# Loading and modulating a second group of rows earlier in a streaming-encoder step

## The chip, the cores and the metric

The kernel runs on one core of one Trainium2 chip. The metric is the device time of one execution in microseconds (us), the median of several runs. Nothing else runs on the chip.

## What is computed

One layer of a hybrid encoder on 1024 prompt rows and 64 sample rows of width 1024, cut here to what the change touches:

```python
sh1, sc1, ga1, sh2, sc2, ga2 = split(silu(c) @ w_ada + b_ada, 6)   # adaLN; one c for the prompt, one for the sample
h   = rmsnorm(x, g_pre_mix) * (1.0 + sc1) + sh1
u   = h @ w_in                      # columns [diff q | diff k | diff v | sb q | sb k | sb v]
mix = concat(differential attention (4 head pairs), stick-breaking attention (8 heads))
x   = x + ga1 * rmsnorm(mix @ w_out, g_post_mix)
x   = x + ga2 * rmsnorm(relu(h2 @ w_up) ** 2 @ w_down, g_post_ffn)  # h2 as h, with sh2 and sc2
```

The keys and values of the new rows are outputs too.

## The kernel before, in words

The 1088 rows are nine tiles of 128 (x0 to x7 of the prompt, x8 the 64 sample rows), in three groups: x0 to x2 are group 0, x3 to x5 group 1, x6 to x8 group 2. All large products run in split form: a number is stored as a high part and a remainder, and one product takes three matmuls (lines 303 to 305: high by high, high by low, low by high).

The first 100 us are the ones that matter here. SyncE (SP) issues all loads on one queue, in this order: `w_ada`, the adaLN weights, of which the first half of the columns is needed here, in four quarters q of four pieces of 512 KB (`ada_raw`, L128; tiles `ar` and `ae`), mixed with x0 to x2 and with three weight tiles of `w_in`; then x3 to x8 (`load_x`, L114, called at L405); then the lambda vectors, two tables (`Tst0`, `T0`) and the next weights (`wq1r`, `wk1r`).

`norm_inplace` (L153) scales a row tile by its inverse RMS: two squares with a sum on ScalarE (L87), three small operations on GpSimd (L89, L80, L81), two multiplications on VectorE (L158). The shift and scale vectors of adaLN come quarter by quarter: each quarter is 16 small matmuls into a bank `pam` (L201), a copy `Rm` to SBUF (L322), four matmuls into `pcm` (L209) and three operations on VectorE that write the columns A1 and B1 (L326 to L328, `columns`). Quarter q gives the columns for the blocks k = 2q and 2q+1, where a block is 128 of the 1024 columns.

`block_T(g, k, tag)` (L330) transposes block k of group g's three row tiles on TensorE into one PSUM bank `px` (`px06` is block 6 of group 0, `px10` block 0 of group 1). `block_mod` (L338) applies A1 and B1 to it (even blocks on VectorE, L346; odd ones on ScalarE, L344) and splits the result into the high part `h1h` (ScalarE, L64) and the remainder `h1l` (L65: on VectorE for group 0, on GpSimd for the others). `first(k)` (L357) multiplies block k of group 0 with the first three weight tiles, nine matmuls into three banks `p00`, `p01`, `p02` that stay open over all eight blocks.

The loop at L383 goes over the four quarters, with the modulation of one quarter running between the matmuls of the next. After it come `first(4)` to `first(7)`, the loads of x3 to x8, the projections of group 0, and then `ready_1` (L579, called at L1006): the norms of x3 to x5 and the eight blocks of group 1. The projections of group 1 (`pq01`, `pk01`, `pv01`) and the first attention steps (`pz`) follow; the blocks of group 2 are made inside the projection of group 1 (`proj`, L563).

The program order isn't the order on the engines: the kernel is built with a scheduler that places each instruction by its own estimate of when its inputs are there. Each engine then executes the order that it was given, and a load on SP first waits for a counter: eight counters are used in turn, so each load waits until the load eight places before it has landed.

A bank is one of two of its tag ("tr", "qk", "pv", "pj"). While `p00` to `p02` are open, each of the first three tags has one bank left, so a `px` has to be read before the next one of its tag can be written.

Of the kernel before, what the change touches and what calls it, by code (L numbers as in the profile page):

```python
# [18 lines left out]
KT = D // P  # L19
# [8 lines left out]
NTT = 9  # L28


def fr(ap):
    return ap.bitcast(F32)


def build(tc, I, O):
    nc = tc.nc
# [10 lines left out]
    def big(name, tag, shape, dt=F32R):  # L47
        return sb.tile(shape, dt, tag=tag, name=name, bufs=BUFS[tag])

    def small(shape, name, tag, dt=F32, bufs=2):  # L50
        return sb.tile(shape, dt, tag=tag, name=name, bufs=bufs)
# [4 lines left out]
    def bank(name, tag):  # L56
        return pp.tile([P, 512], F32, tag=tag, name=name)
# [4 lines left out]
    def split(src, hi, lo, eh=None, el=None):  # L62

        (eh or nc.scalar.copy)(hi, src)  # L64
        (el or nc.vector).tensor_tensor(lo, src, fr(hi), ALU.subtract)  # L65

    def halves(name, n=2):
        return [big(f"{name}_{i}", "s", [P, 512], F32) for i in range(n)]
# [9 lines left out]
    def rstd(ss, rows, name, add=EPS, inv=1.0 / D):  # L78
        r = small([P, 1], name, "rs", bufs=4)
        nc.gpsimd.tensor_scalar(r[:rows], ss, inv, add, ALU.mult, ALU.add)  # L80
        nc.gpsimd.tensor_tensor(r[:rows], r[:rows], mhalf[:rows], ALU.pow)  # L81
        return r

    def sumsq(srcs, rows, name, scratch):
        ss = small([P, 2], name, "ss", bufs=4)
        for i, (a, jk) in enumerate(zip(srcs, scratch)):
            nc.scalar.activation(jk[:rows, : a.shape[-1]], a, AF.Square, accum_out=ss[:rows, i : i + 1])  # L87
        if len(srcs) == 2:
            nc.gpsimd.tensor_tensor(ss[:rows, 0:1], ss[:rows, 0:1], ss[:rows, 1:2], ALU.add)  # L89
        return ss[:rows, 0:1]  # L90
# [5 lines left out]
    def x_rows(m):  # L96
        return (x_p[m * P : (m + 1) * P, :], P) if m < 8 else (x_s, TS)
# [16 lines left out]
    def load_x(m):  # L114
        src, rows = x_rows(m)
        x = big(f"x{m}", "qk" if m < 8 else "v", [P, 1024], F32)
        load(x[:rows], src)
        return [x[:, :512], x[:, 512:]]
# [9 lines left out]
    def ada_raw(q, part, half):  # L128
        n = 4 * q + 2 * part + half
        if n < 10:  # L130
            raw = big(f"ar{q}{part}{half}", "qk", [P, 4, 256], F32)
        else:
            raw = eh[(n - 10) // 3][:, (n - 10) % 3]
        c0 = D * part + 256 * q
        load(raw, w_ada[:, 4 * half : 4 * half + 4, c0 : c0 + 256])
        ada_raws[c0, half] = raw
# [9 lines left out]
    xn = []  # L146
# [6 lines left out]
    def norm_inplace(xs, m):  # L153
        rows = x_rows(m)[1]
        jk = [small([P, 512], f"jk{m}{i}", "ah") for i in range(2)]
        r = rstd(sumsq([x[:rows] for x in xs], rows, f"ssa{m}", jk), rows, f"rsa{m}")
        for x in xs:
            nc.vector.tensor_scalar(x[:rows], x[:rows], r[:rows], None, ALU.mult)  # L158
# [126 lines left out]
    def drain(gen):  # L285
        for _ in gen:
            pass
# [10 lines left out]
    def dense_T(ps, w, act, g, ks=range(KT)):  # L298

        n = GRP[g][1]  # L300
        (wh, wl), (hh, hl) = w, act[g]
        for k in ks:
            mm(ps[:, :n], lhsT=wh[:, k, :], rhs=hh[:, k, :n], start=(k == 0), stop=False)  # L303
            mm(ps[:, :n], lhsT=wh[:, k, :], rhs=hl[:, k, :n], start=False, stop=False)  # L304
            mm(ps[:, :n], lhsT=wl[:, k, :], rhs=hh[:, k, :n], start=False, stop=(k == 7))  # L305
            yield 3 * n / 2400
# [4 lines left out]
    def proj_weights(u, i):  # L311
        c = unit_cols(u)[i]
        return weights(w_in[:, :, c : c + P], [P, KT, P], f"w{'qkv'[i]}{u}", el=nc.vector if u == 0 else None)
# [16 lines left out]
    def block_T(g, k, tag):  # L330

        ps = bank(f"px{g}{k}", tag)
        for m in range(3 * g, 3 * g + 3):
            rows, off = x_rows(m)[1], (m % 3) * P
            nc.tensor.transpose(ps[:, off : off + rows], xn[m][k // 4][:rows, (k % 4) * P : (k % 4 + 1) * P], ident[:rows, :rows])
        return ps

    def block_mod(ps, g, k, el=None, on_act=False):  # L338
        n = GRP[g][1]
        xt = small([P, 512], f"xt{g}{k}", "al")  # L340
        for j, c in ((0, slice(0, min(n, TP - GRP[g][0]))), (1, slice(256, 320)))[: 1 + (g == 2)]:
            a, b = A1[:, k, j : j + 1], B1[:, k, j : j + 1]
            if on_act and j == 0:
                nc.scalar.activation(xt[:, c], ps[:, c], AF.Identity, bias=b, scale=a)  # L344
            else:
                nc.vector.tensor_scalar(xt[:, c], ps[:, c], a, b, ALU.mult, ALU.add)  # L346
        hi, lo = (t[:, k, :n] for t in hT[g])
        split(xt[:, :n], hi, lo, el=el)
        if g == 2:
            nc.vector.tensor_tensor(hT[g][0][:, k, 320:384], xt[:, 256:320], fr(hi[:, 256:320]), ALU.subtract)  # L350
# [6 lines left out]
    def first(k):  # L357

        for i in range(3):
            drain(dense_T(PS[i], PW[0, i], hT, 0, (k,)))  # L360
# [6 lines left out]
    def first_weights(half, up=False):  # L367
        ks = slice(4 * half, 4 * half + 4)
        for i in range(3):
            c = unit_cols(0)[i]  # L370
            if up:
                load(w0[i][:, ks], w_in[:, ks, c : c + P])
                continue
            split(w0[i][:, ks], *(t[:, ks] for t in PW[0, i]), el=nc.vector)

    for q in range(4):
        for part, half in ((0, 0), (0, 1), (1, 0), (1, 1)):
            if q + part:
                ada_raw(q, part, half)
        if q < 2:  # L380
            first_weights(q, True)
    pend = []
    for q in range(4):  # L383
# [16 lines left out]
        elif q >= 1:  # L400
            first(2 * q - 2)
            first(2 * q - 1)
    for k in range(4, KT):
        first(k)
    xn += [load_x(m) for m in range(3, NTT)]  # L405


    lam4 = small([P, 4, 64], "lam4", "ah")
# [154 lines left out]
    def proj(u, g):  # L563
        for i, f in enumerate((proj_q, proj_k, proj_v)):
            if (u, i) not in PW:
                PW[u, i] = proj_weights(u, i)
            for n, c in enumerate(f(u, g, PW[u, i])):
                yield c

                if u == 0 and g == 1:  # L570
                    n += (0, 8, 17)[i]
                    if n >= 5 and (n - 5) % 2 == 0 and (n - 5) // 2 < KT:
                        k = (n - 5) // 2
                        block_mod(block_T(2, k, "tr"), 2, k, nc.gpsimd, k % 2 == 1)
                        yield 0.4
            if g == 2 and u < 7:
                PW[u + 1, i] = proj_weights(u + 1, i)

    def ready_1():  # L579
        for m in range(3, 6):  # L580
            norm_inplace(xn[m], m)
        for k in range(KT):
            block_mod(block_T(1, k, "tr"), 1, k, nc.gpsimd, k % 2 == 1)

# [416 lines left out]
            need.append((steps.index(st), (u, g)))  # L1003
    cost = [st.cost for st in steps]
    drain(proj(0, 0))
    ready_1()  # L1006
    for m in range(6, 9):
        norm_inplace(xn[m], m)
    rows = chain(gate_rows(2 * D, I["g_post_mix"], "r1", 0, ("s", "s")), mod2)
# [63 lines left out]
    for m in range(NTT):  # L1073
# [25 lines left out]
        xn = halves(f"xn{m}")  # L1099
# [196 lines left out]
```

## Time and profile before

| | |
|---|---|
| median of 3 runs | 1566.44 us (1564.3 to 1569.17) |
| the profiled execution | 1567.92 us, span 1566.2 us |
| mean granted TensorE clock | 0.986 |
| TensorE busy | 1504.5 us, 96% of the span |
| VectorE, ScalarE, GpSimd busy | 917.5, 704.6, 331.0 us |

The span is the time from the first to the last instruction. TensorE is busy nearly throughout, from 700 us (the end of the attention; the output projection and the feed-forward part follow) on without a gap to about 1500 us. What it loses lies in the first 100 us and in the second half of the attention (400 to 700 us). A time that TensorE doesn't lose early moves everything behind it forward only if the work behind waits for TensorE.

### The profile page before, as it was taken

Reading aid. Unit: us, or ns where it says so; the run is one execution under the profiler, and the core shown is the slowest. Engines: PE = TensorE matmul, PEld = TensorE weight load, DVE = VectorE, ACT = ScalarE, POOL = GpSimd, SP = SyncE. Lnnn points to the kernel's source line nnn. Section 1 sums busy time; section 2 is a strip of 40 time slices with the busy share of each in tenths; the row PEclk is TensorE's granted clock in tenths of the full one; section 3 lists DMA queues with packets and bytes.
Section 4 is the critical chain, followed back from the end, with each engine's and each line's share of the span. In section 5 each row is a group of like instructions: output and inputs, shape, how many; then the busy total and the mean of one; then the engine's idle time right before and its main releaser. Section 6 shows DMA issues by size and latency. Waiting matters only on the chain.

```text
span 1566.2 us, 23554 instructions
## 1 busy us (share of the span) xinstructions
PE 1504.5 (96%) x8714; PEld 1343.9 (86%) x8714; DVE 917.5 (59%) x1784; ACT 704.6 (45%) x1665; POOL 331.0 (21%) x516
## 2 busy tenths in 40 slices
PE   5899999999999999879999999999999999999998
PEld 3689898989989888768899888899899899899896
DVE  3776768676768576875453454444554544544447
ACT  3766766667676575956564122212122111221132
POOL 1453443535152322521110000000000000000002
PEclk9999999999999999989999999999999999999999
DMA  9422342423232214354221222111111011111025
GB/s 303 127 61 83 93 126 85 131 93 108 66 97 74 83 53 126 109 162 152 75 61 41 68 81 81 55 54 41 54 55 41 28 40 54 54 52 43 28 81 181
DMA packets 152516, 133.20 MB, mean 85 GB/s; under 512 B 11233, under 2 KB 136274, under 8 KB 152402
## 3 DMA queue, kind: packets, MB, share of 16 engines
q1 hardware_dynamic: 152402, 131.71, 27.2%
q8 instruction: 68, 1.11, 0.3%
q14 instruction: 46, 0.38, 0.1%
HBM read 108.59 MB, written 23.09 MB: 84 GB/s over the span
## 4 chain that ended last, share of the span: by engine, by line
PE 84%; DVE 5%; ACT 3%; issue 3%; POOL 1%; DMA 1%; DVEq 0%; POOLq 0%; ACTq 0%
PE pu L303 8%; PE pu L305 8%; PE pu L304 8%; PE pd L1171 8%; PE pd L1172 8%; PE pd L1174 7%; PE pt L604 2%; PE py L1085 2%; PE py L1086 2%; PE pq L303 2%; PE pq L304 2%; PE pq L305 2%; PE py L1088 2%; PE pk L304 2%; PE pk L303 2%
## 5 line engine op out<-in xcount | busy, mean ns | idle before, releaser
L1178 DVE TENSOR_TENSOR acc<-pd,acc 128x512 f32<-128x512 f32 x252 | 171.8, 687 | 113.1 <-PE pd L1174 107.4
L1156 ACT ACTIVATE sq<-pu 128x384 f32<-128x384 f32 (+1 forms) x96 | 45.2, 470 | 309.6 <-PE pu L305 309.6
L1157 DVE TENSOR_TENSOR sq<-sq 128x384 f32<-128x384 f32 (+1 forms) x96 | 72.4, 754 | 173.2 <-ACT sq L1156 173.2
L65 DVE TENSOR_TENSOR al<-pt,ah 128x512 fp32r<-128x512 f32 (+2 forms) x128 | 75.8, 600 | 32.4 <-ACT ah L64 31.1
L64 ACT CAST ah<-pt 128x512 fp32r<-128x512 f32 (+2 forms) x128 | 65.9, 521 | 29.3 <-PE pt L604 23.8
L593 PE MATMUL pz<-K,Q 128*128 128x512 f32 (+2 forms) x192 | 72.6, 381 | 6.6 <-DVE mn L678 1.9
L604 PE MATMUL pt<-ident,s 128*128 128x128 f32 x432 | 70.5, 278 | 0.6 <-issue 0.4
L594 PE MATMUL pz<-Kl,qz 128*128 128x512 f32 (+2 forms) x192 | 66.7, 353 | 0.0
L642 ACT ACTIVATE s<-s,mn 128x512 f32<-128x512 f32 (+3 forms) x96 | 58.6, 612 | 15.8 <-DVE mn L678 14.6
L743 DVE TENSOR_TENSOR_SCAN s<-k,s 128x128 f32<-128x128 f32 (+1 forms) x64 | 53.8, 849 | 13.3 <-ACT k L767 7.3
L65 DVE TENSOR_TENSOR rl<-sq,rh 128x384 fp32r<-128x384 f32 x64 | 35.7, 558 | 37.8 <-ACT rh L64 37.8
L766 ACT ACTIVATE s<-pz 128x512 f32<-128x512 f32 (+2 forms) x96 | 48.0, 500 | 20.2 <-PE pz L594 15.0
L789 PE MATMUL po<-al,V 128*128 128x256 f32 (+1 forms) x160 | 43.1, 304 | 14.3 <-DVE al L65 14.1
L604 PEld LDWEIGHTS pt<-ident,s 128*128 128x128 f32 x432 | 50.3, 142 | 4.0 <-DVE s L743 0.6
L442 POOL CAST qz<-Q 64x256 fp32r<-64x256 f32 x64 | 29.9, 468 | 105.1 <-PE pz L594 93.6
L593 PEld LDWEIGHTS pz<-K,Q 128*128 128x128 f32 x192 | 36.7, 191 | 17.0 <-DVE mn L678 5.9
L64 ACT CAST rh<-sq 128x384 fp32r<-128x384 f32 x64 | 32.8, 513 | 40.2 <-DVE sq L1157 38.2
L767 ACT ACTIVATE k<-pz 128x512 f32<-128x512 f32 (+2 forms) x96 | 47.9, 499 | 1.4 <-DVE s L743 0.8
L789 PEld LDWEIGHTS po<-al,V 128*128 128x128 f32 x160 | 31.2, 195 | 18.8 <-DVE al L65 18.0
L788 PE MATMUL po<-ah,V 128*128 128x256 f32 (+1 forms) x160 | 45.0, 292 | 0.3 <-DVE ok L467 0.3
L743 DVE TENSOR_TENSOR_SCAN s<-k,s,s 128x512 f32<-128x512 f32 x32 | 43.3, 1353 | 0.4
L64 ACT CAST r<-sq 128x320 fp32r<-128x320 f32 x32 | 14.8, 461 | 62.9 <-DVE sq L1157 62.9
(1232 smaller groups left out, 5135.4 us busy)
## 6 DMA issues: line engine op xcount, KB each, us to landing
arr<-in_w_ada SPq DMA_DIRECT2D x16, 512.0 KB
arm<-in_w_ada SPq DMA_DIRECT2D x16, 512.0 KB
ar<-in_w_ada SPq DMA_DIRECT2D x10, 512.0 KB
mixD<-mx SPq DMA_DIRECT2D x32, 128.0 KB
xr<-in_x_prompt SPq DMA_DIRECT2D x16, 256.0 KB
xD<-xr SPq DMA_DIRECT2D x16, 256.0 KB
xy<-xD SPq DMA_DIRECT2D x8, 512.0 KB
out_y_prompt<-xy SPq DMA_DIRECT2D x16, 256.0 KB
```

The costliest lines, as they stand in the source:

```text
L64: (eh or nc.scalar.copy)(hi, src)
L65: (el or nc.vector).tensor_tensor(lo, src, fr(hi), ALU.subtract)
L303: mm(ps[:, :n], lhsT=wh[:, k, :], rhs=hh[:, k, :n], start=(k == 0), stop=False)
L304: mm(ps[:, :n], lhsT=wh[:, k, :], rhs=hl[:, k, :n], start=False, stop=False)
L305: mm(ps[:, :n], lhsT=wl[:, k, :], rhs=hh[:, k, :n], start=False, stop=(k == 7))
L593: mm(ps[:, :w], lhsT=S["Q"][m][:, qt], rhs=S["Kd"][m][:, c0 : c0 + w], start=True, stop=False)
L604: nc.tensor.transpose(pt[:kr, i * P : (i + 1) * P], a, ident)
L743: nc.vector.tensor_tensor_scan(d, k, d, 0.0 if c == n - 1 else s[c + 1][:, 0:1], ALU.mult, ALU.add)
L1171: mm(ps, lhsT=rh[:, off : off + P], rhs=wh[:, cols], start=(j == 0), stop=False)
L1172: mm(ps, lhsT=rh[:, off : off + P], rhs=wl[:, cols], start=False, stop=(m == 8 and end))
L1174: mm(ps, lhsT=rl[:, off : off + P], rhs=wh[:, cols], start=False, stop=end)
L1178: nc.vector.tensor_tensor(acc[m][:, cols], ps, acc[m][:, cols], ALU.add)
```

## The change

Three edits, all in the first 100 us. Before the last quarter's four `w_ada` pieces, x3 to x5 are loaded. The norms of x3 to x5 are made inside the loop, after quarter 2. The eight blocks of group 1 follow directly on `first(4)` to `first(7)`, on the three tags in turn, where they were made after the projections of group 0 on the tag "tr" alone; `ready_1` goes. The lambda loads stand behind the new code in the program.

```diff
     for q in range(4):
+        if q == 3:
+            xn += [load_x(m) for m in range(3, 6)]
         for part, half in ((0, 0), (0, 1), (1, 0), (1, 1)):
             if q + part:
                 ada_raw(q, part, half)
...
             first(2 * q - 2)
             first(2 * q - 1)
-    for k in range(4, KT):
-        first(k)
-    xn += [load_x(m) for m in range(3, NTT)]
+        if q == 2:
+            for m in range(3, 6):
+                norm_inplace(xn[m], m)
+    xn += [load_x(m) for m in range(6, NTT)]
+    for k in range(KT):
+        if k < 4:
+            first(4 + k)
+        block_mod(block_T(1, k, ("tr", "qk", "pv")[k % 3]), 1, k, nc.gpsimd, k % 2 == 1)
...
-    def ready_1():
-        for m in range(3, 6):
-            norm_inplace(xn[m], m)
-        for k in range(KT):
-            block_mod(block_T(1, k, "tr"), 1, k, nc.gpsimd, k % 2 == 1)
...
     drain(proj(0, 0))
-    ready_1()
     for m in range(6, 9):
         norm_inplace(xn[m], m)
```

Since a scheduler sets the order, three places show what the edits do to it. The first is SyncE, the loads around the last quarter; `ae0` and `ae1` hold the pieces of `w_ada` from the eleventh on, of which the last four belong to quarter 3, and the counters of the loads are DMAHW0 to DMAHW7. Before:

```order
L135 DMA ae0_78<-in_w_ada 128x4x256 [waits DMAHW0_49]
L135 DMA ae1_79<-in_w_ada 128x4x256 [waits DMAHW1_49]
L135 DMA ae1_79<-in_w_ada 128x4x256 [waits DMAHW2_49]
L135 DMA ae1_79<-in_w_ada 128x4x256 [waits DMAHW3_49]
L117 DMA x3_457<-in_x_prompt 128x1024 [waits DMAHW4_49,PE_49]
L117 DMA x4_459<-in_x_prompt 128x1024 [waits DMAHW5_49,PE_49]
L117 DMA x5_461<-in_x_prompt 128x1024 [waits DMAHW6_49,PE_49]
L117 DMA x6_463<-in_x_prompt 128x1024 [waits DMAHW7_49,PE_49]
L117 DMA x7_465<-in_x_prompt 128x1024 [waits DMAHW0_49,PE_49]
L117 DMA x8_467<-in_x_sample 64x1024 [waits DMAHW1_49]
L410 DMA lam4_469<-in_lambda_q1 128x64 [waits DMAHW2_49,Activation_49]
```

And now:

```order
L117 DMA x3_197<-in_x_prompt 128x1024 [waits DMAHW0_49,PE_49]
L117 DMA x4_199<-in_x_prompt 128x1024 [waits DMAHW1_49,PE_49]
L117 DMA x5_201<-in_x_prompt 128x1024 [waits DMAHW2_49,PE_49]
L135 DMA ae0_78<-in_w_ada 128x4x256 [waits DMAHW3_49]
L135 DMA ae1_79<-in_w_ada 128x4x256 [waits DMAHW4_49]
L135 DMA ae1_79<-in_w_ada 128x4x256 [waits DMAHW5_49]
L135 DMA ae1_79<-in_w_ada 128x4x256 [waits DMAHW6_49]
L117 DMA x6_460<-in_x_prompt 128x1024 [waits DMAHW7_49,PE_49]
L117 DMA x7_462<-in_x_prompt 128x1024 [waits DMAHW0_49,PE_49]
L117 DMA x8_464<-in_x_sample 64x1024 [waits DMAHW1_49]
L880 DMA Tst0_1752<-in_dist_s 128x64 [waits DMAHW2_49]
L668 DMA T0_670<-in_dist 128x1024 [waits DMAHW3_49,DVE_49]
```

x3 to x5 have taken the places of the last quarter's first three pieces, and the last quarter those behind; x6 to x8 stand where they stood. The four lambda loads no longer follow x8: `Tst0`, `T0`, `wq1r` and `wk1r` do.

The second place is VectorE, from the copy of the last quarter's bank (`Rm3`) to the remainders of group 0's last two blocks. Before:

```order
L322 COPY Rm3_403<-pam3_368 128x512
L65 TENSOR_TENSOR h1l0_116<-xt04_383,h1h0_115 128x384
L326 TENSOR_TENSOR A1_121<-pcm3_405,colE_112 128x4
L327 TENSOR_TENSOR B1_122<-pcm3_405,colE_112 128x4
L328 SCALAR_TENSOR_TENSOR A1_121<-A1_121,colE_112 128x4
L346 TENSOR_SCALAR xt06_413<-px06_360,A1_121,B1_122 128x384
L158 TENSOR_SCALAR x3_457<-x3_457,rsa3_544 128x512 x2
L65 TENSOR_TENSOR h1l0_116<-xt06_413,h1h0_115 128x384
L65 TENSOR_TENSOR h1l0_116<-xt07_417,h1h0_115 128x384
```

And now:

```order
L322 COPY Rm3_442<-pam3_407 128x512
L158 TENSOR_SCALAR x6_460<-x6_460,rsa6_641 128x512 x2
L158 TENSOR_SCALAR x7_462<-x7_462,rsa7_652 128x512 x2
L326 TENSOR_TENSOR A1_121<-pcm3_444,colE_112 128x4
L327 TENSOR_TENSOR B1_122<-pcm3_444,colE_112 128x4
L158 TENSOR_SCALAR x8_464<-x8_464,rsa8_663 64x512 x2
L328 SCALAR_TENSOR_TENSOR A1_121<-A1_121,colE_112 128x4
L346 TENSOR_SCALAR xt06_452<-px06_399,A1_121,B1_122 128x384
L421 TENSOR_TENSOR lam4_566<-lam4_566 128x64 x2
L65 TENSOR_TENSOR h1l0_116<-xt07_456,h1h0_115 128x384
L65 TENSOR_TENSOR h1l0_116<-xt06_452,h1h0_115 128x384
```

The norms of x6, x7 and x8 stand now ahead of the third operation on the last quarter's columns, and so ahead of blocks 6 and 7 of group 0; before, the norm of x3 alone stood near them. On ScalarE the six squares of x6 to x8 stand likewise ahead of block 7 and of the high parts of blocks 6 and 7.

The third place is TensorE, around the last quarter's `pcm3`. Before:

```order
L335 MATMUL px07_364<-ident_66,x0_1_87 128x128 [waits DVE_49]
L335 MATMUL px07_364<-ident_66,x1_1_93 128x128
L335 MATMUL px07_364<-ident_66,x2_1_99 128x128
L303 MATMUL p00_156<-h1h0_115,w00h_167 128x384 [waits Activation_49]
L303 MATMUL p01_157<-h1h0_115,w10h_169 128x384
L303 MATMUL p02_158<-h1h0_115,w20h_171 128x384
L209 MATMUL pcm3_405<-sel_85,Rm3_403 128x2 [waits DVE_49]
L209 MATMUL pcm3_405<-sel_85,Rm3_403 128x2 x3
```

And now:

```order
L209 MATMUL pcm3_444<-sel_85,Rm3_442 128x2 [waits DVE_49]
L209 MATMUL pcm3_444<-sel_85,Rm3_442 128x2 x3
L335 MATMUL px11_492<-ident_66,x3_197 128x128 [waits Activation_49]
L335 MATMUL px11_492<-ident_66,x4_199 128x128
L335 MATMUL px11_492<-ident_66,x5_201 128x128
L335 MATMUL px10_475<-ident_66,x3_197 128x128 [waits DVE_49]
L335 MATMUL px10_475<-ident_66,x4_199 128x128
L335 MATMUL px10_475<-ident_66,x5_201 128x128
L303 MATMUL p00_156<-h1h0_115,w00h_167 128x384 [waits Activation_49]
L303 MATMUL p01_157<-h1h0_115,w10h_169 128x384
```

`pcm3` stood inside `first(4)`; it now follows `first(5)`. Behind it stand two blocks of group 1, `px11` and `px10`, each waiting for the reader of the bank that it takes (`px07` and `px06`), and only then `first(6)`.

## Rows read from the trace of the kernel before

**Rows 1.** Busy time by stage: us, length, busy time of each engine (instructions), clock, DMA share, GB/s

```profile
20.00:30.00 10.00, 8.76 (x55) 5.58 (x56) 4.77 (x12) 3.60 (x7) 0.00 (x0) 0.66 1.07 350
51.00:84.00 33.00, 26.61 (x144) 21.87 (x143) 24.55 (x62) 24.39 (x65) 19.01 (x31) 0.95 0.15 43
62.00:66.00 4.00, 3.88 (x17) 3.38 (x16) 3.69 (x13) 2.80 (x10) 2.64 (x4) 0.57 0.00 0
100.00:400.00 300.00, 295.20 (x1981) 271.17 (x1981) 211.31 (x599) 205.17 (x595) 127.37 (x206) 1.00 0.35 104
400.00:700.00 300.00, 273.87 (x1773) 246.86 (x1772) 220.38 (x364) 200.86 (x460) 99.15 (x146) 0.95 0.32 97
```

**Rows 2.** Timeline of TensorE, 39 to 61 us: start, length, instruction [idle before <- releaser]

```profile
39.61 0.64 PE L201 MATMUL pam<-ae,sc 128*32 128x256 f32 x8
40.18 1.05 PE L209 MATMUL pcm<-sel,Rm 128*128 128x2 f32 x8
...
42.59 0.55 PE L335 MATMUL px<-ident,x 128*128 128x128 f32 x3
43.42 0.44 PE L303 MATMUL p<-h1h,w00h 128*128 128x384 f32 x1 [0.28 <-ACT h1h L64]
...
44.21 1.05 PE L209 MATMUL pcm<-sel,Rm 128*128 128x2 f32 x8
...
47.84 0.42 PE L303 MATMUL p<-h1h,w00h 128*128 128x384 f32 x1
...
51.05 0.38 PE L335 MATMUL px<-ident,x 128*128 128x128 f32 x2
...
54.91 0.33 PE L593 MATMUL pz<-K,Q 128*128 128x128 f32 x1 [1.42 <-ACT K L513]
...
60.40 0.44 PE L303 MATMUL pq<-h1h,w00h 128*128 128x384 f32 x1 [2.01 <-ACT h1h L64]
```

**Rows 3.** Timeline of SyncE's queue, 37 to 50 us (a row is an issue)

```profile
37.45 0.58 SPq L117 DMA_DIRECT2D x<-in_x_sample  x1
39.01 0.33 SPq L410 DMA_DIRECT2D lam<-in_lambda_q  x1
40.44 0.33 SPq L410 DMA_DIRECT2D lam<-in_lambda_k  x1
41.72 0.33 SPq L410 DMA_DIRECT2D lam<-in_lambda_q  x1
43.00 0.33 SPq L410 DMA_DIRECT2D lam<-in_lambda_k  x1
44.27 0.33 SPq L879 DMA_DIRECT2D Tst<-in_dist_s  x1
46.27 0.33 SPq L667 DMA_DIRECT2D T<-in_dist  x1
48.78 0.38 SPq L294 DMA_DIRECT2D wq1r<-in_w_in  x1
49.90 0.38 SPq L294 DMA_DIRECT2D wk1r<-in_w_in  x1
```

**Rows 4.** Timeline of ScalarE: the squares of x5, and a table load

```profile
47.75 0.63 ACT L87 ACTIVATE jk<-x 128x512 f32<-128x512 f32 x1
...
49.04 0.19 ACT L87 ACTIVATION_READ_ACCUMULATOR jk<-x 128x1 f32 x1
...
56.84 1.28 ACT L416 ACT_TABLE_LOAD   x1
```

**Rows 5.** Timeline of GpSimd: the sum of x5's squares, and a remainder of group 1

```profile
49.31 0.19 POOL L89 TENSOR_TENSOR ssa<-ssa 128x1 f32<-128x1 f32 x1 [0.87 <-ACT jk L87]
...
55.71 1.00 POOL L65 TENSOR_TENSOR h1l<-xt,h1h 128x384 fp32r<-128x384 f32 x1 [0.43 <-ACT h1h L64]
```

**Rows 6.** Timeline of VectorE: block 6 of group 0, and the norm of x5

```profile
45.69 0.68 DVE L346 TENSOR_SCALAR xt<-px,A,B 128x384 f32<-128x384 f32 x1
...
50.44 0.90 DVE L158 TENSOR_SCALAR x<-x,rsa 128x512 f32<-128x512 f32 x2 [1.09 <-POOL rsa L81]
```

## The prediction

> **What bounds the kernel now.** I read the stages first. From 100 to 400 us TensorE is busy 295.2 of 300 us at full clock, so there a microsecond lost or won earlier is simply carried on; from 400 to 700 it waits 26.1 us and runs at 0.95 of the clock [rows 1]. The change lies in the first 100 us, where from 51 to 84 us TensorE waits 33 - 26.61 = 6.39 us, and from 62 to 66 us it runs at a granted clock of 0.57, which costs 4 x 0.43 = 1.72 us [rows 1]. The reader should see in TensorE's timeline what it waits for: up to 51.05, while group 0 is multiplied, it hardly stops (0.28 us at 43.42). Behind that it stops for 1.42 us (54.91, a cast of K) and 2.01 us (60.40, a high part of group 1) [rows 2]. So group 1 comes too late, and the change goes at that. The ledger of what is lost from 39 to 84 us: 0.28 + 6.39 + 1.72 = 8.4 us. The change can win no more than this, and what it loses new is to be set against it.
>
> SyncE's queue tells when loads land, since each load waits for the one eight places before it. x8's issue at 37.45 follows the landing of the last quarter's second piece, the four lambda loads those of the third (39.01), the fourth (40.44), x3 (41.72) and x4 (43.00), `Tst0` that of x5 (44.27), `T0` x6 (46.27), `wq1r` x7 (48.78) and `wk1r` x8 (49.90) [rows 3]. Pieces of 512 KB land 1.28 us apart up to x5, x6 and x7 2.0 and 2.5 us apart.
>
> **The change, part by part.** No matmul, load or vector operation is added or taken away; all is order, and so waits.
>
> *The last quarter's weights.* x3 to x5 take the places of its first three pieces, so its four pieces land at the times of the places they now have: 40.44, 41.72, 43.00 and 44.27. TensorE is there at 39.61 as before, waits 0.83 us, does the first piece (0.57) and `pcm2` (1.05), is at 42.05, does the second piece (0.5) and waits from 42.55 to 43.00 for the third, 0.45. Then come that piece (0.5), two blocks of transposes of 0.55 each and the fourth piece (0.5): `first(4)` begins at 45.1 (43.42 before) [rows 2, 3]. The norms of x3 to x5 don't move this: x5 lands at 39.01; two squares take 47.75 to 49.23, that is 1.48 us, and from there to the end of the norm on VectorE (51.34) it is 2.11 us [rows 4 to 6]. So VectorE is free at 39.01 + 1.48 + 2.11 = 42.6, `pcm2` ends at 42.05, and from the end of `pcm2` to `first(4)` it was 2.19 us (41.23 to 43.42): 44.8, before TensorE is there. **New waits: 1.3 us.** They are certain within some tenths.
>
> *The last two blocks of group 0.* `first(4)` and `first(5)` take 47.84 - 43.42 less 1.0 for the `pcm3` between them, 3.4 us, so they end at 48.5, and `pcm3` at 49.55 [rows 2]. Before, block 6 was on VectorE 0.4 us after `pcm3` (45.69). Now VectorE has the norms of x6 to x8 ahead of the third operation on these columns, ScalarE their six squares ahead of block 7, and TensorE stands at `px11` and `px10`, whose banks are freed by blocks 7 and 6. Bound from below: x6 to x8 keep the pace of 1.28 us, x6 at 45.55, x7 at 46.83; the squares then run without a gap to 45.55 + 3 x 1.48 = 49.99, the norm of x8 ends 2.11 later at 52.10, and the column operation and block 6 (0.16 and 0.68, [rows 6] for the second) end at 52.95: TensorE waits 3.4 us. Bound from above: they land as they did; squares 46.27 to 47.75, 48.78 to 50.26 and on to 51.74, norm at 53.85, block 6 at 54.7: 5.15 us. I take the middle, **4.3 us**, since x6 to x8 keep their places but what follows them in the queue is other. `first(6)` would start near 55, some 7 us later than at 47.84. The matmuls of group 0 that were covered before lose their cover here.
>
> *Group 1.* Its blocks start right behind, and this is what the change wins: transposes and norms are done, and the 6.39 us of waits from 51 to 84 us shrink. While TensorE does `first(6)` and `first(7)` (3.2 us, 47.84 to 51.05) and two blocks of transposes (1.1), ScalarE does two lambda sums, the table load (1.28), block 1 and the first high part, and GpSimd the first remainder (1.00) [rows 2, 4, 5]; the first projection of group 1 then hardly waits. Per block TensorE needs six matmuls (3.2/3 = 1.07 us) and 0.55 of transposes, GpSimd 1.00, so TensorE should be the slower one; but on ScalarE the copies of group 0's three banks stand between the high parts of blocks 2 and 3. Bounds: 0, and the 2.01 us of the like wait at 60.40 [rows 2]. I take **1.0 us**.
>
> *The clock.* In the trace, TensorE's wait at 60.40 was followed by 0.57 of the clock; the wait of 1.42 us at 54.91 was not, for 33 us x 0.05 = 1.65 us is all that the whole stretch lost, and 62 to 66 us hold 1.72 of it [rows 1, 2]. From 20 to 30 us the granted clock was 0.66, a loss of 3.4 us. The new wait of 3.4 to 5.15 us is longer than that of 2.01, so I expect one stretch at half clock again, at about 56 us instead of 62. Bounds 0 and 3.4; I take **1.7 us**, as at 62 to 66 us. The Trainium skill, page "TensorE: Matmul & The Clock Gate", Part 1, says that the default state is the throttled one and activity releases it. That speaks against the change, as it makes a break in the middle of group 0's matmuls; by that rule the sum stands as it is, without it 1.7 us less; the trace shows both a wait with and one without a fall.
>
> **Sum:** 1.3 + 4.3 + 1.0 + 1.7 = 8.3 us lost from 39 to 84 us, where 8.4 were lost before: a difference of -0.1 us, so no change. With all lower bounds it is 1.3 + 3.4 = 4.7, -3.7 us; with all upper ones 1.3 + 5.15 + 2.0 + 3.4 = 11.85, +3.5 us. The sum is made against the profiled execution, 1567.92 us (a span of 1566.2 and 1.7 us around it), which is 1.5 us above the median of the runs shown; so I say 1566.4 for the median. Behind 100 us the order of each engine shifts in many small places, since the scheduler follows the new start; there are 4.8 us of waits between 100 and 400 us, and I allow half of them, 2.4 us, either way. That makes -6.1 to +5.9.
>
> **The rivals.** *Group 1 is fully covered (faster).* The clock doesn't fall, group 1 never waits, x6 to x8 land at pace, and half of the waits up to 400 us go with it: -6.1 us, 1560.3. For it: these are the waits that the trace names. Against it: all three lucky ends are needed, and the order puts x8's norm ahead of block 6 whatever the loads do.
>
> *The tables and weights slow x6 to x8 (slower).* `T0`, `wq1r` and `wk1r`, three loads of 512 KB, were issued at 46.27 to 49.90, behind the lambda loads that waited; now they follow `Tst0` directly and their counters are free by 43.00, so they are in the queue while x6 to x8 land. If the three share the engines with these, x8 lands up to 3 x 1.28 = 3.84 us later than 49.90, the wait at `px11` is 5.15 + 3.84 = 9.0, with the longer clock loss of 3.4 the sum is 1.3 + 9.0 + 1.0 + 3.4 = 14.7: +6.3 us, 1572.7. It decides from 52.1 us on: an x8 landed 2.2 us late gives +4.7. For it: x6 and x7 landed 2.0 and 2.5 us apart though little was queued behind them [rows 3]. Against it: up to x5 the landings follow the order of issue at an even pace. The Trainium skill, "DMA: Bandwidth & Descriptors", section "Queues, rings and completion order", says that on each DMA engine the descriptors of one queue are consumed in ring order; by that rule later loads can't slow earlier ones, and this rival falls away. The trace is for it up to x5 and leaves it open behind.
>
> *The clock holds.* The forecast without the 1.7 us: 1564.7, within the bound of no change. That the edits don't take effect can be left out: the order shows the moves.
>
> **Chances.** The forecast 0.64 and the clock that holds 0.08, both "same" (a measurement of this kernel can tell about 0.3%, 4.7 us, from no change); group 1 fully covered 0.14, faster; slowed loads 0.14, slower. The range takes in both bounds with the 2.4 us of the later stages: 1560.5 to 1572.5, which cuts the two outer cases about in half.
>
> **What would show it.** Right: `pam` waits for `ae` (none did); VectorE's x6 to x8 norms before a `first(6)` that starts at 54 to 56 us; a wait of 3 to 5 us of TensorE at `px11`, released by ScalarE; a stretch of about 0.57 of the clock at 55 to 60 us; group 1's `pq` then with waits of about 1 us, and the first matmul of group 2's `pq02` at about 84 us as before. Wrong: a `first(6)` before 52 us, no fall of the clock, or waits between 100 and 700 us that differ by more than 2.4 us.

## The result, and the profile after

The changed kernel takes **1588.46 us** (median, 1585.96 to 1591.65), the kernel before 1566.11 beside it on the same chip: a ratio of 1.0136, 95% interval 1.0119 to 1.0153. It is 22 us slower. "No change" was wrong, and the time lies 16 us outside the range. The profiled execution has a span of 1589.9 us (1566.2 before) and a mean granted clock of 0.975 (0.986 before).

The first line of the page shows how the 23.7 us of span divide:

```profile
PE 1516.0 (95%) x8714; PEld 1356.4 (85%) x8714; DVE 926.1 (58%) x1784; ACT 704.6 (44%) x1665; POOL 329.3 (21%) x516
```

TensorE does the same 8714 matmuls, but is busy 11.5 us longer with them (1516.0 against 1504.5), and it stands still 12.2 us longer (1589.9 - 1516.0 = 73.9 against 1566.2 - 1504.5 = 61.7). So half of the loss is waits and half is longer busy time, at a mean clock that is lower. The stages of after (columns as in [rows 1]) tell where:

```profile
39.00:84.00 45.00, 38.16 (x239) 33.77 (x239) 28.67 (x83) 31.28 (x79) 19.80 (x35) 0.92 0.32 95
51.00:84.00 33.00, 29.73 (x166) 27.45 (x167) 22.73 (x69) 25.35 (x64) 16.11 (x25) 0.90 0.08 22
54.00:58.00 4.00, 4.00 (x16) 4.00 (x15) 2.30 (x7) 3.86 (x11) 0.44 (x1) 0.50 0.00 0
62.00:66.00 4.00, 4.00 (x30) 3.95 (x29) 2.10 (x4) 3.85 (x9) 2.38 (x3) 1.00 0.00 0
100.00:400.00 300.00, 286.40 (x1853) 262.05 (x1854) 203.45 (x569) 188.74 (x553) 115.88 (x196) 0.96 0.32 96
400.00:700.00 300.00, 270.19 (x1779) 246.26 (x1778) 217.72 (x347) 200.05 (x464) 107.97 (x159) 0.95 0.29 86
```

The first of these stages in before:

```profile
39.00:84.00 45.00, 38.32 (x234) 31.57 (x234) 31.47 (x80) 33.16 (x87) 22.16 (x40) 0.96 0.35 112
```

From 51 to 84 us TensorE waits 3.27 us where it waited 6.39 [rows 1]. That looks like the gain that was sought, but its longest wait now begins at 48.08, ahead of that window: from 39 to 84 us it waits 6.84 us, where it waited 6.68. The half-clock stretch has moved from 62 to 66 us (now at full clock) to around 54 to 58, and it has grown: from 51 to 84 us the clock costs 33 x 0.10 = 3.3 us, where it cost 1.7. The stage from 100 to 400 us, which ran without a loss before (295.20 busy at full clock, [rows 1]), now has 13.6 us of idle time and a clock of 0.96. TensorE's timeline of the early stage answers to [rows 2]:

```profile
41.84 0.64 PE L201 MATMUL pam<-ae,sc 128*32 128x256 f32 x8 [0.60 <-DMA ae<-in_w_ada]
...
47.13 0.95 PE L209 MATMUL pcm<-sel,Rm 128*128 128x2 f32 x8
53.61 1.54 PE L335 MATMUL px<-ident,x 128*128 128x128 f32 x6 [5.53 <-ACT xt L344]
54.80 0.67 PE L303 MATMUL p<-h1h,w00h 128*128 128x384 f32 x1
...
80.52 0.31 PE L303 MATMUL pq<-h1h,w00h 128*128 128x320 f32 x1
```

`pam` waits for `ae`, `px11` waits 5.53 us behind the norms of x6 to x8, `first(6)` starts at 54.80, and the third group's `pq02` begins at 80.52, where it was 83.76 before. That isn't a lead of 3 us: `pq02` now stands earlier in the order, with 388 matmuls of TensorE ahead of it where 399 were. At 84 us TensorE has begun 409 matmuls, 401 before, so up to here the two are about level. Then the changed kernel falls behind. The first projection matmul of unit 1, `pq10`, stands 3.5 us later than before (107.6 to 111.1), that of unit 2, `pq20`, 8.9 (166.2 to 175.1), `pq40` 19.9 (308.2 to 328.1), `pq60` 26.0 (473.1 to 499.1), and behind that the distance grows no more (23.7 at the end).

Where the first large waits behind the early stage arise is seen from 96 to 105 us, in VectorE's, GpSimd's and TensorE's timelines of after:

```profile
96.07 3.11 DVE L701 SCALAR_TENSOR_TENSOR s<-s,cf,s 128x512 f32<-128x512 f32 x2
...
100.68 1.94 DVE L645 TENSOR_TENSOR l<-l 128x1 f32<-128x1 f32 x1
...
96.46 2.57 POOL L65 TENSOR_TENSOR wq1l<-wq1r,wq1h 128x1024 fp32r<-128x1024 f32 x1 [3.50 <-ACT wq1h L64]
...
100.24 2.36 POOL L65 TENSOR_TENSOR wk1l<-wk1r,wk1h 128x1024 fp32r<-128x1024 f32 x1 [0.55 <-ACT wk1h L64]
...
99.33 0.30 PE L605 MATMUL pt<-ident,s 128*128 128x128 f32 x1 [1.74 <-DVE s L701]
...
104.67 0.80 PE L594 MATMUL pz<-K,Q 128*128 128x512 f32 x1 [2.68 <-DVE Q L496]
```

A pair of VectorE's operations on `s` takes 3.11 us (1.15 at 105.75) and a sum of single columns 1.94 us, whose median is 0.159. Both end within 0.2 us of the end of a GpSimd weight split beside them (99.03 and 102.60). TensorE waits 1.74 us, and its clock falls to the lower of its two levels (1.2 of 2.4 GHz); its wait of 2.68 us comes while it is there:

```profile
100.00:104.00 4.00, 1.70 (x3) 0.79 (x3) 3.97 (x8) 3.22 (x10) 3.55 (x4) 0.52 0.56 143
104.00:108.00 4.00, 3.33 (x12) 3.28 (x13) 2.70 (x8) 0.23 (x1) 0.61 (x1) 0.50 0.34 127
```

Before, the same two splits ran at 96.04 and 99.12 too; but beside them VectorE mostly had operations that read PSUM (the one sum of single columns there took 0.57 us), and TensorE waited 0.74 us at most. The operations are the same; what stands beside what is not. Hence two candidates: the order of the attention stages, or the later norms and blocks that put its chain behind.

### The profile page after: what moved, and what is told of

It reads as the page before. It is cut to its first block, busy times and chain, and to the rows that moved or that the text cites. A ratio compares the mean times of both kernels' runs of the same rounds, so it can differ in the third digit from the quotient of the medians.

```text
span 1589.9 us, 23580 instructions
## 1 busy us (share of the span) xinstructions
PE 1516.0 (95%) x8714; PEld 1356.4 (85%) x8714; DVE 926.1 (58%) x1784; ACT 704.6 (44%) x1665; POOL 329.3 (21%) x516
## 4 chain that ended last, share of the span: by engine, by line
PE 82%; DVE 6%; ACT 3%; issue 3%; DMA 3%; POOL 1%; SPq 1%; POOLq 0%; DVEq 0%; ACTq 0%
PE pu L303 8%; PE pu L305 8%; PE pu L304 8%; PE pd L1171 8%; PE pd L1172 8%; PE pd L1174 7%; PE pt L605 2%; PE pq L303 2%; PE py L1086 2%; PE py L1085 2%; PE pq L304 2%; PE pq L305 2%; PE py L1088 2%; PE pk L303 2%; PE pk L305 2%
## 5 line engine op out<-in xcount | busy, mean ns | idle before, releaser
L1178 DVE TENSOR_TENSOR acc<-pd,acc 128x512 f32<-128x512 f32 x252 | 171.8, 687 | 113.3 <-PE pd L1174 107.6
L1156 ACT ACTIVATE sq<-pu 128x384 f32<-128x384 f32 (+1 forms) x96 | 45.1, 470 | 309.0 <-PE pu L305 309.0
L767 ACT ACTIVATE s<-pz 128x512 f32<-128x512 f32 (+2 forms) x96 | 48.4, 504 | 22.3 <-PE pz L595 15.3
L679 DVE CUSTOM_DVE_ANT_0 s<-pz,T 128x512 f32<-128x512 f32 (+3 forms) x64 | 37.2, 586 | 13.0 <-PE pz L595 12.4
```

What stands on the lines that cost most here:

```text
L1178: nc.vector.tensor_tensor(acc[m][:, cols], ps, acc[m][:, cols], ALU.add)
```

## The experiments

Theory A: the scheduler lays out the attention anew for a start with other times, and that order makes the loss. Theory B: the early edit itself puts the attention chain behind. Theory C: GpSimd's weight splits hold up VectorE; from e9 on it is written C'. (Where an expectation calls `pq10` and `pq70` transposes, the first projection matmuls of units 1 and 7 are meant.)

**A neutral edit (e1).** In the kernel before, the lambda block moves up; nothing else.

```
+    lam4 = small([P, 4, 64], "lam4", "ah")
+    ...
     pend = []
     for q in range(4):
```

> The kernel before with one edit that has nothing to do with rows or blocks: the four small lambda loads and their arithmetic are written ahead of the loop over the adaLN quarters. The scheduler answers with a third order of the attention stages: between the first transposes pq10 and pq70 some 1295 of 2540 TensorE rows stand otherwise than before, 1237 otherwise than in the changed kernel. Theory A (the order that the scheduler lays out behind 100 us makes the loss): this order is worth more than 3 us of difference in one direction or the other, so under 1563 or over 1569 us, with all of the difference between 90 and 600 us. Theory B (the early edit itself, rows and norms of x6 to x8 ahead of the first group's last blocks, puts the attention chain behind): nothing early has changed here, so 1564 to 1568 us. Theory C (GpSimd's weight splits lengthen VectorE's work where the two meet): only where a split of 128x1024 meets VectorE's short operations; 1564 to 1568 unless such a meeting is seen.

Measured: 1590.47 us, ratio 1.0147 (1.0120 to 1.0173). An edit that leaves rows, norms and blocks alone costs as much as the change. B can't explain this. A holds in the main: 3.7 of the 22 us lie behind 806 us, not between 90 and 600 (the table of stages below).

**The blocks back (e2, the first diff), the loads back (e3, the second).** Both start from the changed kernel.

```
-        block_mod(block_T(1, k, ("tr", "qk", "pv")[k % 3]), 1, k, nc.gpsimd, k % 2 == 1)
...
     drain(proj(0, 0))
+    for k in range(KT):
+        block_mod(block_T(1, k, "tr"), 1, k, nc.gpsimd, k % 2 == 1)
```

```
-        if q == 3:
-            xn += [load_x(m) for m in range(3, 6)]
...
-        if q == 2:
-            for m in range(3, 6):
-                norm_inplace(xn[m], m)
-    xn += [load_x(m) for m in range(6, NTT)]
+    xn += [load_x(m) for m in range(3, NTT)]
+    for m in range(3, 6):
+        norm_inplace(xn[m], m)
```

> The changed kernel, but the second group's transposes and modulation stand where they stood before (behind the first unit's projections); loads of x3 to x5 ahead of the last quarter and their norms stay as changed. From pq10 to pq70 its TensorE rows are the very same as in e1. Theory A: the time of e1 within 3 us. Theory B: the loads and norms are as early as in the changed kernel and those of x6 to x8 follow at once, so most of the loss stays: over 1580 us, whatever e1 gives.

> The changed kernel without the early loads: x3 to x8 are loaded behind the last quarter of the adaLN weights as before, the norms of x3 to x5 and the second group's blocks stand directly behind the first group's. About 100 of 2540 TensorE rows between pq10 and pq70 differ from e1 and e2. Theory A: within 5 us of e1. Theory B: the blocks now wait for later rows; the stage up to 84 us is 2 to 6 us longer than in the changed kernel, and the loss behind it stays: over 1588 us.

Measured: e2 1587.24 us (1.0111; 1.0078 to 1.0145), 3.2 us off e1, about what A said (3 us); it fits B as well, so it decides nothing alone. e3 1578.49 us (1.0076; 1.0053 to 1.0098), 12 us less than e1: a miss for both theories. But these 12 us don't lie where the rows of the two were compared: from `pq10` to `pq70` e3 takes 463.7 us and e1 462.9, and e3 is 5.7 us ahead at `pq10` and gains the rest behind `pq70` (the table of stages below). TensorE stands still 71.3 us in e3 (1575.7 - 1504.4) and 71.8 in e1 (1588.0 - 1516.2): the waits are the same in sum, and the difference lies in its busy time (mean clock 0.985 against 0.981).

**Another order by idle work (e8), and its control (e13).** In the kernel before, ahead of `drain(proj(0, 0))`, 12 transposes in e8 and 4 in e13:

```
+    pxd = bank('pxd', 'tr')
+    for i in range(12):
+        nc.tensor.transpose(pxd[:, :P], ident, ident)
```

> The kernel before with 12 transposes of 128x128 that nobody reads, behind the first group's blocks (12 x 0.3 us at most, 3.6 us; none if they fall into a wait). The scheduler answers with a fourth order: 983 of some 2540 rows between pq10 and pq70 stand otherwise than before. Theory A: over 3.6 us, more than the transposes take, the time is off by what the new order is worth: 1572 us or more, or 1562 or less, with the difference between 90 and 600 us. Theories B and C: 1566 to 1570 us.

> The kernel before with 4 idle transposes of 128x128 at the place where e8 has 12. Here the order stays: no row differs from before's between pq10 and pq70. Theory A: the transposes themselves cost 4 x 0.3 us at most, so 1565 to 1569 us, and the other 18 us of e8 belong to its order. If instead the bank and the moment at which the transposes sit make the loss, as a wait that starts everything later, 4 of them should show it as well: over 1575 us.

Measured: e8 1586.30 us (1.0119; 1.0096 to 1.0141); its twelve transposes took 1.47 us at 47.37. e13 1568.0 us (1.0004; 0.9993 to 1.0014). Four transposes leave the order as it is and cost nothing that can be measured; twelve change it and cost some 18 us. The stage from 84 to 500 us of before, e13, e8 and e1, in this order:

```profile
84.00:500.00 416.00, 407.63 (x2738) 373.06 (x2737) 299.27 (x756) 287.75 (x786) 166.75 (x269) 1.00 0.31 92
```

```profile
84.00:500.00 416.00, 407.41 (x2721) 373.14 (x2720) 298.22 (x754) 287.03 (x785) 166.45 (x268) 1.00 0.31 92
```

```profile
84.00:500.00 416.00, 397.64 (x2617) 361.60 (x2616) 288.55 (x738) 274.11 (x756) 162.07 (x260) 0.98 0.31 91
```

```profile
84.00:500.00 416.00, 395.45 (x2621) 360.91 (x2619) 285.14 (x736) 273.17 (x755) 161.41 (x260) 0.99 0.31 91
```

The two with before's order wait 8.4 and 8.6 us here, the other two 18.4 and 20.6 us at a lower clock, with 100 or more matmul records fewer in the same 416 us.

**The change with the order held (e5, e6).** The scheduler's time simulation is switched off in both kernels; behind the first 223 TensorE rows they agree on all engines.

```
-    with tile.TileContext(nc, schedule_with_timeline_sim=True) as tc:
+    with tile.TileContext(nc, schedule_with_timeline_sim=False) as tc:
```

> The kernel before with the scheduler's time simulation switched off, so that the engines get their instructions by the order of the code. An order of its own everywhere, so its time against the kernel before says nothing of the change: anywhere from 1570 to 1700 us. It is the base for e6: behind the first 223 TensorE rows the two differ in no row on any engine.

> The changed kernel with the scheduler's time simulation switched off. Theory A (the loss is another order of the attention stages, which the scheduler laid out because the start had other times): with the order behind the start the same as in e5, the change is worth what it does up to 84 us, minus 3 us by the two traces, so between 5 us less and 2 us more than e5. Theory B (the rows and norms ahead of the first group's last blocks put the attention chain behind): the loss is there without another order, 10 to 25 us more than e5, built up between 84 and 500 us.

Measured: 1647.88 us (1.0517; 1.0490 to 1.0544) and 1647.46 us (1.0519; 1.0490 to 1.0548). With one order the change is worth nothing that can be measured. Four of TensorE's waits in e5, and the same four in e6:

```profile
119.80 0.33 PE L604 MATMUL pt<-ident,s 128*128 128x128 f32 x1 [2.31 <-DVE s L700]
...
255.15 0.33 PE L621 MATMUL po<-V,al 128*128 128x128 f32 x1 [1.01 <-DVE al L65]
...
488.85 0.90 PE L551 MATMUL pdv<-ident,df 128*128 128x128 f32 x3 [4.02 <-POOL df L540]
...
722.77 0.88 PE L604 MATMUL pt<-ident,s 128*128 128x128 f32 x6 [1.57 <-DVE s L743]
```

```profile
116.49 0.47 PE L605 MATMUL pt<-ident,s 128*128 128x128 f32 x1 [2.31 <-DVE s L701]
...
252.55 0.33 PE L622 MATMUL po<-V,al 128*128 128x128 f32 x1 [1.01 <-DVE al L65]
...
486.10 0.90 PE L558 MATMUL pdv<-ident,df 128*128 128x128 f32 x3 [4.02 <-POOL df L547]
...
720.90 0.87 PE L605 MATMUL pt<-ident,s 128*128 128x128 f32 x6 [1.56 <-DVE s L744]
```

The waits are the same to 0.01 us, and the changed kernel reaches them 3.31, 2.60, 2.75 and 1.87 us earlier. What this lead of single traces is worth isn't shown: up to the first of these waits TensorE stood still equally long (30.8 us in e5, 31.0 in e6), and the medians are 0.4 us apart. But nothing in the early edit puts the attention behind. The written order is 80 us slower than the scheduler's and has more slack (112.0 us of idle time in e5), which alone would leave room for B; with the loss in e1 and e8, where the early edit is missing, **B is out.**

**Splits on VectorE (e4, e7, e9 to e12).** The edit for units 1 to 7 (21 operations of 128x1024 change their engine), in after (e4), before (e7), e1 (e9) and e5 (e10):

```
-        return weights(..., el=nc.vector if u == 0 else None)
+        return weights(..., el=nc.vector)
```

e11 is after with `if u < 2`; e12 is e7 with the 16 splits of the cached values on VectorE too.

> The changed kernel with the weight splits of units 1 to 7 on VectorE in place of GpSimd (some 21 x 2 operations of 128x1024 that move engine; the order behind 100 us changes too, 1336 of 2540 rows from before, 1555 from after). Theory C: the waits of 1.7 and 2.7 us at 99 and 105 us, where VectorE's operations took 3.11 and 1.94 us beside GpSimd's splits, are gone, and with them half of the loss: 1568 to 1580 us. Theory A: the time is set by the new order, so this tells little about the size: no operation of VectorE of that line longer than 1.2 us, but waits elsewhere. Theory B: no change, over 1583 us.

> The kernel before with the weight splits of units 1 to 7 on VectorE in place of GpSimd. Its order behind pq10 differs from before's (1065 of some 2540 rows by the first count). Theory C (GpSimd's splits lengthen VectorE's work): without them the kernel before gains too, 2 to 8 us, 1558 to 1564 us. Theory A: another order, and the time goes with it: more than 3 us off in a direction that can't be told, with the chance that it is slower, since VectorE gets some 23 us more of work.

> The kernel of e1 (lambda loads early, 22 us slower than before) with the weight splits of units 1 to 7 on VectorE. A third order with the splits there: 768 of some 2520 rows off e7's, 554 off e4's. Theory C' (with the splits on GpSimd an order is cheap only where no SBUF operation of VectorE on TensorE's path falls beside a split; without them any order is near 1562): 1558 to 1566 us, and no tensor_tensor_scan of 128x512 beyond 1.4 us. Theory A alone (each order has a time of its own, the splits have no part in it): e4 and e7 were two draws, a third could as well lie at 1575 to 1590 us.

> The kernel of e5 (written order, 1647.9 us) with the weight splits of units 1 to 7 on VectorE. The order hardly changes: 107 of 2540 TensorE rows between pq10 and pq70. Theory C': 5 us or more less than e5, as 4 to 8 us went where the scheduler's time simulation is on. Theory A alone: VectorE gets 21 more operations of 128x1024, some 23 us of work, and the time stays within 3 us of e5 or gets longer.

> The changed kernel with the splits of unit 1's three weights alone on VectorE, those that in the changed kernel lay beside VectorE's 3.11 and 1.94 us operations at 96 to 103 us. The order changes as well (1663 of some 2540 rows off the changed kernel's, 950 off before's). Theory C': the waits of 1.7 and 2.7 us at 99 and 105 us are gone, the later ones beside splits of units 2 to 7 stay: 1570 to 1583 us. Theory A alone: a draw like the others, 1575 to 1590 us with the waits at 99 to 107 us of the same size.

> The kernel before with the weight splits of units 1 to 7 and the 16 splits of the cached values (128x512, 1373 ns each on GpSimd) on VectorE: whether a version beats both kernels by more than e7. Theory C': 1554 to 1562 us. Theory A alone: anything from 1556 to 1590 us.

| run | us | ratio to before (95%) |
|---|---|---|
| e4, after | 1562.56 | 0.9968 (0.9955 to 0.9981) |
| e7, before | 1561.42 | 0.9952 (0.9940 to 0.9965) |
| e9, e1's edit | 1571.07 | 1.0021 (1.0011 to 1.0030) |
| e10, written order | 1629.86 | 1.0402 (1.0384 to 1.0420) |
| e11, after, unit 1 alone | 1573.51 | 1.0042 (1.0028 to 1.0057) |
| e12, before, cache too | 1568.51 | 1.0011 (1.0001 to 1.0022) |

e10 is the clean one: in an order that hardly changes, the move of the splits saves 18.0 us against e5. In e5 the wait at 119.80 comes from this pair, first VectorE's row, then GpSimd's:

```profile
116.88 2.87 DVE L700 SCALAR_TENSOR_TENSOR s<-s,cf,s 128x128 f32<-128x128 f32 x1
...
117.26 2.33 POOL L65 TENSOR_TENSOR wv1l<-wv1r,wv1h 128x1024 fp32r<-128x1024 f32 x1
```

In e10 both are VectorE's, and TensorE's `pt` behind them no longer waits:

```profile
114.31 0.56 DVE L700 SCALAR_TENSOR_TENSOR s<-s,cf,s 128x128 f32<-128x128 f32 x1
...
114.80 1.21 DVE L65 TENSOR_TENSOR wv1l<-wv1r,wv1h 128x1024 fp32r<-128x1024 f32 x1
```

By line, the 48 operations on `s` (shortest, median and longest in ns) in before, after, e5 and e10:

```profile
L700 DVE SCALAR_TENSOR_TENSOR s<-s,cf,s x48: 340/742/1219, 66.2 to 346.7; 128x512 f32<-128x512 f32 x24, 128x128 f32<-128x128 f32 x8, 128x256 f32<-128x256 f32 x8, 128x384 f32<-128x384 f32 x8
```

```profile
L701 DVE SCALAR_TENSOR_TENSOR s<-s,cf,s x48: 336/747/2479, 71.4 to 365.7; 128x512 f32<-128x512 f32 x24, 128x128 f32<-128x128 f32 x8, 128x256 f32<-128x256 f32 x8, 128x384 f32<-128x384 f32 x8
```

```profile
L700 DVE SCALAR_TENSOR_TENSOR s<-s,cf,s x48: 341/738/2869, 79.0 to 383.0; 128x512 f32<-128x512 f32 x24, 128x128 f32<-128x128 f32 x8, 128x256 f32<-128x256 f32 x8, 128x384 f32<-128x384 f32 x8
```

```profile
L700 DVE SCALAR_TENSOR_TENSOR s<-s,cf,s x48: 342/676/769, 78.3 to 375.3; 128x512 f32<-128x512 f32 x24, 128x128 f32<-128x128 f32 x8, 128x256 f32<-128x256 f32 x8, 128x384 f32<-128x384 f32 x8
```

C has a price, then: e10 shows it, e7 came as C expected (1558 to 1564), and e4 went below its 1568 to 1580, though a wait of 1.80 us is left at 99.24. e9 and e12 missed what C expected (1558 to 1566 and 1554 to 1562), e9 also with a scan of 128x512 of 1.81 us on VectorE where 1.4 was the limit, and e9 is 10 us behind e7. Where that lies is told by the start of three matmuls in the trace of each run: the first of `pq10`, of `pq70` and of `pu`, with which the feed-forward part begins.

| run | splits of units 1 to 7 on | `pq10` starts, us | `pq10` to `pq70` | `pq70` to `pu` | `pu` to the end |
|---|---|---|---|---|---|
| before | GpSimd | 107.6 | 452.7 | 227.7 | 778.2 |
| e13, before's order | GpSimd | 109.1 | 453.5 | 227.9 | 778.2 |
| after | GpSimd | 111.1 | 474.2 | 226.4 | 778.2 |
| e1 | GpSimd | 113.6 | 462.9 | 229.6 | 781.9 |
| e2 | GpSimd | 116.0 | 465.4 | 228.1 | 778.2 |
| e3 | GpSimd | 107.9 | 463.7 | 225.8 | 778.3 |
| e8 | GpSimd | 111.2 | 465.4 | 228.5 | 778.4 |
| e4, after | VectorE | 110.9 | 446.1 | 225.6 | 778.2 |
| e7, before | VectorE | 105.5 | 445.6 | 225.9 | 778.3 |
| e9, e1's edit | VectorE | 110.8 | 446.4 | 227.3 | 781.9 |

From `pq10` to `pq70` the five new orders with the splits on GpSimd take 10 to 22 us longer than before's. With the splits on VectorE the three starts, that of before, that of after and that of e1, come within 0.8 us of each other. So in this stage the difference between the orders went with the splits. It went out of VectorE's delays, not out of GpSimd's queue: of TensorE's waits here VectorE ends 8.8 us in before, 13.8 to 17.9 in the five new orders and 5.7 to 7.3 with the splits on VectorE, while GpSimd ends 1.1 to 2.8 us throughout. The reservation is that each is a single trace, and that moving the splits redraws the order too; but with the order held, from e5 to e10, 15.3 of the 17.0 us of span lie in this stage as well (499.2 to 483.9). e9's 10 us against e7 lie elsewhere: 5.3 ahead of `pq10`, and 3.6 from `pu` on, where e1 has them too. Their cause stays open.

The dear orders also show such meetings at their first long waits. In e1, the rows of VectorE, GpSimd and TensorE:

```profile
99.18 1.72 DVE L643 TENSOR_TENSOR l<-l 128x1 f32<-128x1 f32 x1
...
98.52 2.37 POOL L65 TENSOR_TENSOR wq1l<-wq1r,wq1h 128x1024 fp32r<-128x1024 f32 x1 [5.27 <-ACT wq1h L64]
...
102.14 0.50 PE L592 MATMUL pz<-K,Q 128*128 128x512 f32 x1 [2.32 <-DVE mn L677]
```

The same sum of single columns took 1.71 us in e2, 1.43 in e3 and 1.33 in e8, each time ending with a split, and TensorE's waits behind them are 2.31, 2.32 and 1.98 us. Before's order has long operations too: one of 1.75 us on single columns begins at 234.87, and TensorE hardly waits behind it (0.16 us at 237.92). What counts is where they fall. These first waits are a few us of the 10 to 22; what the rest consists of was not followed wait by wait.

e11 has VectorE's operations short again (1.18 us for the pair on `s`), and `pt` waits 0.18 us, but `pz` still waits 1.80 us at 102.06, behind VectorE's own split of 1.22 us. Its time lies where C expected it (1570 to 1583), but its 15 us can't be told from another order.

**e7 and e4 beat both kernels**: e7 by 0.35 to 0.60%, e4 by 0.19 to 0.45%.

## Why the prediction was wrong

- *The last quarter's weights, 1.3 us of waits.* The wait for `ae` came, once and with 0.60 us; `first(4)` began at 43.90, not 45.1.
- *The wait at `px11`, 4.3 us, bounds 3.4 to 5.15.* 5.53 us, over the upper bound, released by ScalarE as said. The place was right: it ended at 53.61, and the prediction's 49.55 + 4.3 gives 53.85. It is longer because TensorE was there earlier, at 48.08.
- *Group 1, 1.0 us.* No wait at its projections; the one wait of TensorE from 55 to 80 us is 0.62 us at 73.74, at a `po`.
- *The clock, 1.7 us.* A half-clock stretch came where it was put, at the long wait (54 to 58 us at 0.50), but it cost 3.3 us from 51 to 84, close to the upper bound of 3.4. The Trainium skill, "TensorE: Matmul & The Clock Gate", Part 1, calls the throttled state the default. The rows above agree at both places: 54 to 58 us at 0.50 behind the wait of 5.53 us, 100 to 104 us at 0.52 behind that of 1.74.
- *The early sum, -0.1 us.* By the prediction's own ledger, 39 to 84 us, 6.84 + 3.3 = 10.1 us were lost where 8.4 were: +1.7 us, within the bounds of -3.7 to +3.5, and most of it the clock. (`pq02`, expected at 84 us, came at 80.52, but with fewer matmuls ahead of it.) Of e5 and e6 the medians are 0.4 us apart. So the part on which the prediction spent its working was right in its places and near in its sum. Two small slips change nothing: the loads land 1.28 us apart only from x3 on (1.56 and 1.43 us for the two ahead of it, [rows 3]), and -6.1 and +5.9 around 1566.4 give 1560.3 to 1572.3.
- *The rivals.* The loads of x6 to x8 were not slowed: ScalarE's six squares run without a gap for data from 45.69 to 50.3. Group 1 was covered, which the faster rival wanted, but the clock fell. No rival had the cause.
- **The step that failed** is one sentence: "Behind 100 us the order of each engine shifts in many small places [...] there are 4.8 us of waits between 100 and 400 us, and I allow half of them, 2.4 us, either way." The price was taken from the waits that before's order has, and for the clock behind 100 us there was no term at all. A new order doesn't scale these waits; it makes its own. From 100 to 400 us idle time went from 4.8 to 13.6 us, and the clock from 1.00 to 0.96, up to 300 x 0.04 = 12 us. The prediction's own sign of being wrong came: from 100 to 700 us the waits grew by 12.5 us (30.9 to 43.4), where 2.4 were allowed. The row that should have warned was the same one: 295.2 of 300 us at full clock is an order with little left to lose. Of the orders that the scheduler gave with all splits on GpSimd, before's (1566, and 1568 in e13) is the best; the others gave 1578.5 (e3), 1586.3 (e8), 1587.2 (e2), 1588.5 (after) and 1590.5 (e1).

So the price of this change is a draw among orders, not of its rows and blocks: shown by e1 and e8 (the loss without the edit), by e13 (the added work without the loss) and by e6 (the edit without the loss). What makes a draw dear between `pq10` and `pq70` is, as far as the traces of e4, e7, e9 and e10 show it, where VectorE's operations meet GpSimd's splits; the prediction had no term for such meetings. What they cost one by one, and what differs outside that stage, stays open.

## What to carry to other kernels

Where a scheduler with a time model lays out the whole program, an early edit redraws everything behind it. Count the rows that change far from the edit, and if a tuned stage is redrawn, put into the range what a redrawn order costs (here 10 to 22 us by the medians side by side, and in all five cases upwards: the stage had little left to lose). To know what an edit itself is worth, measure it with the order held, as e5 and e6 do, and take a neutral edit that redraws the order as its control. Then look for what makes the orders differ, stage by stage: moving GpSimd's weight splits to VectorE brought before to 1561.4 us and after to 1562.6.

## What the runs showed of the hardware

VectorE's operations with both inputs in SBUF don't slow down in proportion beside a GpSimd split of 128x1024; the small ones end when it ends. The 128x128 operation took 2.87 us in e5 and 0.56 in e10, and ended at 119.75, the split at 119.59. In before and after, the 128x512 operations that take `pz` from PSUM kept their 0.68 us beside splits. The Trainium skill, "SBUF — State Buffer", section "SBUF: two separate sides", says that VectorE and GpSimd share one port pair by an exclusive lock, which an operation of VectorE with two SBUF inputs needs against a GpSimd operation that reads SBUF, and that the loser blocks fully. The trace agrees with this. It doesn't show by the start times who came first: in e5 VectorE's row begins at 116.88, ahead of the split's at 117.26, and still ends behind it. The same split took 2.33 us on GpSimd and 1.21 on VectorE, so moving it also makes it shorter.

Waits can be paid twice: in after, TensorE's idle time grew by 12.2 us and its busy time, for the same matmuls, by 11.5. They need not be: in e3 idle time grew by 9.6 us (71.3 against 61.7) and busy time not at all (1504.4 against 1504.5).
